# Layer norm of a convolution module: the channel tiles are added on GpSimd and VectorE, and TensorE sums one tile over the partitions instead of eight

## The chip, the core and the metric

The kernel runs on one core of one Trainium2 chip. The metric is device microseconds from the start to the end of one execution, the median of several runs. The profile is one execution of its own, recorded by the hardware profiler; its times are microseconds from the start of the span.

## What is computed

The reference is a decoder trunk of two layers on one sequence of 512 positions and 1024 channels. Layer 0 mixes state-space heads and attention heads; layer 1 is a causal convolution module; each ends in a gated FFN. The change touches the convolution module of layer 1 alone:

```python
def layer_norm(x, g, b):
    mu = jnp.mean(xf, -1, keepdims=True)
    var = jnp.mean(jnp.square(xf - mu), -1, keepdims=True)
    y = (xf - mu) * lax.rsqrt(var + EPS)
    return y * g + b

def conformer_conv(h, w1, b1, w_dw, b_dw, ln_g, ln_b, w2, b2):
    a, gt = jnp.split(h @ w1 + b1, 2, axis=-1)
    u = a * jax.nn.sigmoid(gt)
    u = causal_depthwise_conv(u, w_dw, b_dw)          # 31 taps
    u = jax.nn.silu(layer_norm(u, ln_g, ln_b))
    return u @ w2 + b2
```

The mean and the variance run over the 1024 channels of each position.

## The kernel before, in words

Everything is held transposed: a tile has 128 channels in its partitions and positions along its free dimension, so 1024 channels are eight tiles k = 0 to 7. A sum over channels is a sum over the partitions and over the eight tiles. Positions are handled in two halves of 256, called H0 (positions 0 to 255) and H1 (256 to 511); a name that ends in `_0` or `_256` belongs to one of them.

Products with weights keep float32 accuracy by splitting: `slab` (L181 to L196) loads 1024 x 256 weights as `raw`, ScalarE rounds them to `hi`, and VectorE or GpSimd takes the rest as `lo`; `products` (L198 to L211) issues hi x hi, lo x hi and hi x lo for each tile. `raw`, `hi` and `lo` have two buffers each, so the slab after next waits until TensorE has finished with a slab, and its DMA until the subtraction has read the old `raw`. A plain float32 matmul stands as two passes in the trace; the names `mu`, `var`, `cps` and `lnr_b` below are of this kind.

The module runs like this. For each pair of channel tiles two slabs of the first matrix (`wp`) are multiplied, ScalarE takes the sigmoid, VectorE forms the gated tile `cu`. SP's DMA queue then writes 16 shifted pieces of it (`shifted`, L948 to L951) into a tile `u`; the queue carries the slab loads in between, in the order of the code. `conv` (L953 to L963) is 32 small matmuls per tile into `cps`, and ScalarE moves the result with its bias to `cv`. The conv of tile k - 2 is issued with tile k; the second halves of tiles 4 to 7 follow after the layer norm of H0 in the code. GpSimd builds the filters (`w`, L914) and, for the slabs of H0 of the second matrix, the `lo` part (`wq_l`, L195).

`layer_norm(c)` (L991 to L1015) works on one half. TensorE multiplies each of the eight `cv` tiles by a constant matrix with 1/1024 everywhere (`meanw`) and accumulates, so that `mu` holds the mean in all partitions (L995). VectorE subtracts it from each tile (L999), ScalarE squares (L1003, into `cvq`), and TensorE sums every square tile over its partitions, two blocks of 128 positions each, into a column `var` (L1005). VectorE then computes the reciprocal root with twelve small operations (L221 to L226, L1008) and a diagonal (L271), TensorE spreads it over the partitions (`lnr_b`, L274), VectorE scales (L1012), ScalarE applies SiLU (L1013) and converts to `ch` (L1014), and VectorE forms the rest `cl` (L1015). `pw2` (L1019 to L1025) multiplies by the second matrix in four slabs per half (`wq`, result `pq`), VectorE adds the result to the residual `xT` (L592) and ScalarE and others gather squares for the next norm (`n3`, sums `n_s`, spread `n_b`). The last FFN begins with `first_banks`: gate and up products of its first slabs (`f_a`, `f_b` from `wf`), first for H0, then for H1.

The order in which an engine's instructions stand is not the order of the code alone: the program is recorded and a list scheduler with a model of the time places each engine's instructions. An edit can so move work that it does not name. On the chip each engine works through its list in order.

## Time and profile before

| | |
|---|---|
| median of 3 runs | 1872.89 us (1870.29 to 1874.12) |
| the profiled execution | 1885.09 us |
| its span in the trace | 1882.8 us |
| TensorE busy | 1774.7 us, 94% of the span |
| VectorE busy | 1046.5 us, 56% |
| ScalarE busy | 693.1 us, 37% |
| GpSimd busy | 430.5 us, 23% |
| mean clock granted to TensorE | 0.972 of full speed |

PE is TensorE's matmuls and PEld its weight loads, DVE is VectorE, ACT ScalarE, POOL GpSimd, SP the engine whose queue issues most DMAs. A busy share is an average over the whole kernel; what an edit in the convolution module is worth is read in its own stretch, about 1290 to 1520 us. The clock granted to TensorE is a share of full speed: 1.00 is 2.4 GHz, 0.50 is 1.2 GHz, and a value between is a mean over a stretch that holds both.

### The profile page before, as it was taken

To read this page: it belongs to the slowest core of one execution; us is meant where nothing else is said; L and a number is where in the kernel's file an instruction comes from. 1 tells how busy PE (TensorE), PEld (TensorE's weight loads), DVE (VectorE), ACT (ScalarE), POOL (GpSimd) and SP (SyncE) were. 2 spreads that over 40 slices of the span, in tenths; PEclk is the share of its full clock that TensorE was granted. 3 is DMA by queue.
4 is the path that set the end of the run, shared out by engine and by line. 5 is a ranking of instruction groups with operands and counts; after the bars stand their busy time and mean duration, and the time that the engine had idled before them with its cause. 6 is when DMAs were issued, how large, how long until landed. Compare 5 with 4: busy or idle time off the path is not lost.

```text
span 1882.8 us, 24868 instructions
## 1 busy us (share of the span) xinstructions
PE 1774.7 (94%) x9735; PEld 1450.0 (77%) x9735; DVE 1046.5 (56%) x1978; ACT 693.1 (37%) x1331; POOL 430.5 (23%) x328
## 2 busy tenths in 40 slices
PE   5897978999999999997999999999999999999998
PEld 3676766777778878777888888897567988888888
DVE  7858687755565565558665664373204743333336
ACT  6333333334545454344421221253214632122225
POOL 1437686422443440003000000013020200000001
PEclk8998989999999999997999999999998999999999
DMA  8354454545444443424555553253640523322223
GB/s 301 102 138 140 141 141 134 137 112 152 123 128 149 133 125 122 124 74 141 181 190 190 188 201 114 79 169 80 180 132 1 169 77 102 101 89 93 87 94 130
DMA packets 232066, 247.84 MB, mean 132 GB/s; under 512 B 13946, under 2 KB 198076, under 8 KB 231949
## 3 DMA queue, kind: packets, MB, share of 16 engines
q1 hardware_dynamic: 220813, 204.31, 36.6%
q0 software_dynamic: 11136, 41.95, 6.8%
q8 instruction: 77, 1.26, 0.3%
q14 instruction: 40, 0.33, 0.1%
HBM read 228.73 MB, written 8.64 MB: 126 GB/s over the span
## 4 chain that ended last, share of the span: by engine, by line
PE 73%; DVE 11%; DMA 7%; ACT 3%; issue 2%; POOL 2%; SPq 1%; DVEq 0%; ACTq 0%; POOLq 0%
PE fd L207 4%; PE fd L208 4%; PE fd L210 4%; PE fg L208 4%; PE fg L207 4%; PE fu L207 4%; PE fu L208 4%; PE fu L210 4%; PE fg L210 4%; PE cps L959 2%; PE s L717 2%; DMA ar<-a_dram 2%; PE wa L207 1%; PE wa L208 1%; PE wa L210 1%
## 5 line engine op out<-in xcount | busy, mean ns | idle before, releaser
L249 POOL TENSOR_TENSOR n_acc<-n_acc,n_q 128x256 f32<-128x256 f32 x32 | 29.7, 929 | 561.8 <-ACT n_q L245 561.7
L207 PE MATMUL fd<-uh,wd_h 128*128 128x512 f32 (+1 forms) x448 | 148.6, 347 | 0.9 <-DVE xT L592 0.9
L195 DVE TENSOR_TENSOR wf_l<-wf_w,wf_h 128x1024 fp32r<-128x1024 f32 x88 | 106.1, 1241 | 74.4 <-ACT wf_h L194 74.4
L208 PE MATMUL fd<-uh,wd_l 128*128 128x512 f32 (+1 forms) x448 | 147.0, 344 | 0.0
L194 ACT CAST wf_h<-wf_w 128x1024 fp32r<-128x1024 f32 x88 | 87.7, 1048 | 115.7 <-PE fd L210 71.9
L208 PE MATMUL fg<-n_h,wf_l 128*128 128x512 f32 x320 | 126.1, 394 | 2.0 <-DVE wf_l L195 2.0
L207 PE MATMUL fg<-n_h,wf_h 128*128 128x512 f32 x320 | 126.3, 395 | 0.7 <-ACT wf_h L194 0.5
L208 PE MATMUL fu<-n_h,wf_l 128*128 128x512 f32 x320 | 124.7, 390 | 0.0
L207 PE MATMUL fu<-n_h,wf_h 128*128 128x512 f32 x320 | 124.6, 389 | 0.0
L172 POOL TENSOR_TENSOR adap<-adap 128x128 f32<-128x128 f32 (+2 forms) x96 | 103.5, 1082 | 4.7
L869 DVE TENSOR_TENSOR fs<-fs,fu 128x512 f32<-128x512 f32 x40 | 27.5, 688 | 130.2 <-PE fu L210 130.2
L743 ACT ACTIVATE s<-s,nm 128x128 f32<-128x128 f32 x192 | 79.4, 415 | 50.7 <-DVE nm L739 40.4
L194 ACT CAST wd_h<-wd_w 128x1024 fp32r<-128x1024 f32 (+1 forms) x64 | 57.1, 941 | 101.2 <-PE fd L210 80.6
L592 DVE SCALAR_TENSOR_TENSOR xT<-fd,mod,xT 128x512 f32<-128x512 f32 (+1 forms) x64 | 39.1, 615 | 98.1 <-PE fd L210 97.8
L207 PEld LDWEIGHTS fd<-uh,wd_h 128*128 128x128 f32 x448 | 84.1, 188 | 12.0 <-DVE xT L592 1.3
L208 PEld LDWEIGHTS fd<-uh,wd_l 128*128 128x128 f32 x448 | 84.2, 188 | 10.5
L210 PE MATMUL fd<-ul,wd_h 128*128 128x512 f32 (+1 forms) x448 | 91.9, 343 | 0.0
L170 POOL TENSOR_TENSOR adap<-adap,cs 128x1024 f32<-128x1024 f32 x32 | 67.6, 2112 | 90.3 <-DMA adap<-in_ada_w 90.2
L195 DVE TENSOR_TENSOR wd_l<-wd_w,wd_h 128x1024 fp32r<-128x1024 f32 (+1 forms) x64 | 67.7, 1090 | 34.7 <-ACT wd_h L194 34.4
L162 DVE SCALAR_TENSOR_TENSOR adaa<-adaw,cs,adaa 128x512 f32<-128x512 f32 x112 | 84.8, 758 | 2.6
L210 PEld LDWEIGHTS fd<-ul,wd_h 128*128 128x128 f32 x448 | 72.9, 188 | 10.6
L210 PE MATMUL fg<-n_l,wf_h 128*128 128x512 f32 x320 | 79.1, 389 | 0.0
(400 smaller groups left out, 4584.5 us busy)
## 6 DMA issues: line engine op xcount, KB each, us to landing
adaw<-in_ada_w POOLq DMA_DIRECT2D x24, 1024.0 KB, 5.7
wf_w<-in_ffn_w_gate SPq DMA_DIRECT2D x22, 1024.0 KB, 5.2
wf_w<-in_ffn_w_up SPq DMA_DIRECT2D x22, 1024.0 KB
adap<-in_ada_w POOLq DMA_DIRECT2D x32, 512.0 KB, 5.5
wd_w<-in_ffn_w_down SPq DMA_DIRECT2D x16, 1024.0 KB, 5.1
wd_w<-in_ffn_w_down SPq DMA_DIRECT2D x16, 768.0 KB, 4.6
wa_w<-in_hy_w_out SPq DMA_DIRECT2D x20, 512.0 KB, 4.1
u<-cu SPq DMA_DIRECT2D x128, 67.5 KB, 2.0
```

The source lines that it names most:

```text
L162: V.scalar_tensor_tensor(acc, ws[k // 4][:, k % 4, :], cs[:, k:k + 1], acc, op0=ALU.mult, op1=ALU.add)
L170: G.tensor_tensor(w3, w3, cs.unsqueeze(2).broadcast_to([P, KT, P]), op=ALU.mult)
L172: G.tensor_tensor(w[:, 0:n], w[:, 0:n], w[:, n:2 * n], op=ALU.add)
L194: S.copy(hi[:, s:e], raw[:, s:e])
L195: eng.tensor_tensor(lo[:, s:e], raw[:, s:e], hi[:, s:e].bitcast(F32), op=ALU.subtract)
L207: PE.matmul(ps[:, cols], hi[:, o(k):o(k) + P], xh, start=k == 0, stop=False)
L208: PE.matmul(ps[:, cols], lo[:, o(k):o(k) + P], xh, start=False, stop=False)
L210: PE.matmul(ps[:, cols], hi[:, o(k):o(k) + P], acts[k][1][:, cols], start=False, stop=k == nk - 1)
L592: V.scalar_tensor_tensor(xT[m][:, cols], ps[:, cols], mod[l][:, go + m:go + m + 1], xT[m][:, cols], op0=ALU.mult, op1=ALU.add)
L717: marks[hp, 0] = marks[hp, 1] = PE.matmul(ps[:, o:o + 2 * wd].rearrange("p (e w) -> p e w", e=2), q, k, start=True, stop=True)
L743: S.activation(s[:, o:o + wd], s[:, o:o + wd], AF.Exp, bias=nm, accum_out=l)
L959: PE.matmul(ps[g * 32:(g + 1) * 32, :], w4[k][:, g * 8 + m, :], u4[k][:, g, t:t + w], start=m == 0, stop=m == 7)
```

## The change

For the mean, each `cv` tile of channels is added into a tile `csum` (one for each half) as soon as ScalarE has written it: tiles 0 to 4 on GpSimd, 5 and 6 on VectorE. TensorE multiplies only `csum` and tile 7 by `meanw`. For the variance, the square tiles lie in pairs of 128 x 512 with three buffers of their own; VectorE adds the second and third pair onto the first (`vacc`), and TensorE sums `vacc` and the fourth pair over the partitions.

```diff
--- before.py
+++ after.py
@@ -941,7 +941,7 @@
     with tc.tile_pool(name="conf", bufs=2) as conf:
         h = nxt.finish(const, g_mix1, mod[1][:, 0:8], XG)
         w1 = a["cv_w_pw1"][0]
-        cv, u4 = {}, {}
+        cv, u4, csum = {}, {}, {}
 
         def shifted(k, u):
 
@@ -961,6 +961,11 @@
             for c in cols:
                 o = cv[k, c.start] = conf.tile([P, T // 2], F32, tag=f"cv{k}_{c.start}", name=f"cv{k}_{c.start}", bufs=1)
                 S.activation(o, ps[:, c.start - cols[0].start:c.stop - cols[0].start], AF.Identity, bias=bdw[:, k:k + 1])
+                if k == 1:
+                    csum[c.start] = conf.tile([P, T // 2], F32, tag=f"csum{c.start}", name=f"csum{c.start}", bufs=1)
+                    G.tensor_tensor(csum[c.start], cv[0, c.start], o, op=ALU.add)
+                elif 1 < k < KT - 1:
+                    (G if k < 5 else V).tensor_tensor(csum[c.start], csum[c.start], o, op=ALU.add)
 
         for j in range(4):
             ws = [slab([(w1[:, o + j * 256:o + (j + 1) * 256], KT, 256)], f"wp{o}_{j}") for o in (0, D)]
@@ -991,19 +996,24 @@
             n, w = c.start, c.stop - c.start
             nb = w // P
             mb = bank("A", f"mu{n}", (P, w))
-            for i, k in enumerate(range(KT)):
-                PE.matmul(mb, meanw, cv[k, n], start=i == 0, stop=i == KT - 1)
+            PE.matmul(mb, meanw, csum[n], start=True, stop=False)
+            PE.matmul(mb, meanw, cv[KT - 1, n], start=False, stop=True)
             vp = bank("C", f"var{n}", (P, nb))
-            for i, k in enumerate(range(KT)):
+            vacc = None
+            for k in range(KT):
                 t = cv[k, n]
                 V.tensor_tensor(t, t, mb, op=ALU.subtract)
-                if i % 2 == 0:
-                    two = tmp.tile([P, T], F32, tag="st_sq", name=f"cvq{k}_{n}")
-                sq = two[:, i % 2 * w:(i % 2 + 1) * w]
-                S.activation(sq, t, AF.Square)
-                for b in range(nb):
-                    PE.matmul(vp[:, b:b + 1], sq[:, b * P:(b + 1) * P], ones[:, 0:1], start=i == 0 and b == 0,
-                              stop=i == KT - 1 and b == nb - 1)
+                if k % 2 == 0:
+                    two = conf.tile([P, T], F32, tag="cvq", name=f"cvq{k}_{n}", bufs=3)
+                S.activation(two[:, k % 2 * w:(k % 2 + 1) * w], t, AF.Square)
+                if k == 1:
+                    vacc = two
+                elif k in (3, 5):
+                    V.tensor_tensor(vacc, vacc, two, op=ALU.add)
+            for i, sq in enumerate((vacc, two)):
+                for b in range(2 * nb):
+                    PE.matmul(vp[:, b % nb:b % nb + 1], sq[:, b * P:(b + 1) * P], ones[:, 0:1], start=i == 0 and b == 0,
+                              stop=i == 1 and b == 2 * nb - 1)
             vv = tmp.tile([P, nb], F32, tag="st_v", name=f"lnv{n}")
             V.tensor_scalar(vv, vp, 1.0 / D, EPS, op0=ALU.mult, op1=ALU.add)
             rb = spread(rsqrt(vv, nb, f"ln{n}"), nb, f"lnr{n}")
```

The scheduler places the rest anew. Three places matter below. TensorE, from the first matmul of conv 7 for H0 (`cps7_0`) to the sums of squares of H0; before:

```order
L959 MATMUL cps7_0_11069<-u4_7_10964,w4_7_10782 32x256
L995 MATMUL mu0_11104<-cv0_0_10426,meanw_9893 128x256
L995 MATMUL mu0_11104<-cv1_0_10538,meanw_9893 128x256
L959 MATMUL cps7_0_11069<-u4_7_10964,w4_7_10782 32x256
L995 MATMUL mu0_11104<-cv2_0_10666,meanw_9893 128x256
L995 MATMUL mu0_11104<-cv3_0_10778,meanw_9893 128x256
L995 MATMUL mu0_11104<-cv4_0_10906,meanw_9893 128x256
L995 MATMUL mu0_11104<-cv5_0_11014,meanw_9893 128x256
L959 MATMUL cps7_0_11069<-u4_7_10964,w4_7_10782 32x256
L995 MATMUL mu0_11104<-cv6_0_11067,meanw_9893 128x256
L959 MATMUL cps6_256_11273<-u4_6_10856,w4_6_10670 32x256
L959 MATMUL cps7_0_11069<-u4_7_10964,w4_7_10782 32x256 x29
```

and now, the same stretch:

```order
L959 MATMUL cps7_0_11080<-u4_7_10973,w4_7_10790 32x256
L999 MATMUL mu0_11115<-csum0_10540,meanw_9893 128x256
L959 MATMUL cps6_256_11274<-u4_6_10864,w4_6_10676 32x256
L959 MATMUL cps7_0_11080<-u4_7_10973,w4_7_10790 32x256
L959 MATMUL cps6_256_11274<-u4_6_10864,w4_6_10676 32x256 x6
L959 MATMUL cps7_0_11080<-u4_7_10973,w4_7_10790 32x256
L959 MATMUL cps6_256_11274<-u4_6_10864,w4_6_10676 32x256 x4
L959 MATMUL cps7_0_11080<-u4_7_10973,w4_7_10790 32x256 x29
L959 MATMUL cps6_256_11274<-u4_6_10864,w4_6_10676 32x256 x17
L1000 MATMUL mu0_11115<-cv7_0_11113,meanw_9893 128x256
L959 MATMUL cps5_256_11238<-u4_5_10734,w4_5_10546 32x256 x32
L959 MATMUL cps7_256_11310<-u4_7_10973,w4_7_10790 32x256 x16
```

The seven calls of `mu` between the conv pieces have become one on `csum0`, conv of H1's tile 6 (`cps6_256`) fills the places between, and `mu`'s last call stands behind 17 conv calls instead of 22; the sums of squares come later in the list, behind conv 5 and half of conv 7 of H1.

VectorE, from H0's diagonal `lnr0_d` on; before:

```order
L271 TENSOR_SCALAR lnr0_d_11165<-cst_72,ln0_y_11153 128x128 x2
L1012 TENSOR_TENSOR cv0_0_10426<-cv0_0_10426,lnr0_b_11168 128x256
L1012 TENSOR_TENSOR cv1_0_10538<-cv1_0_10538,lnr0_b_11168 128x256
L1012 TENSOR_TENSOR cv2_0_10666<-cv2_0_10666,lnr0_b_11168 128x256
L1012 TENSOR_TENSOR cv3_0_10778<-cv3_0_10778,lnr0_b_11168 128x256
L1012 TENSOR_TENSOR cv4_0_10906<-cv4_0_10906,lnr0_b_11168 128x256
L1012 TENSOR_TENSOR cv5_0_11014<-cv5_0_11014,lnr0_b_11168 128x256
L1012 TENSOR_TENSOR cv6_0_11067<-cv6_0_11067,lnr0_b_11168 128x256
L1012 TENSOR_TENSOR cv7_0_11102<-cv7_0_11102,lnr0_b_11168 128x256
L999 TENSOR_TENSOR cv0_256_10428<-cv0_256_10428,mu256_11351 128x256
```

and now, the same stretch:

```order
L271 TENSOR_SCALAR lnr0_d_11164<-cst_72,ln0_y_11152 128x128 x2
L1005 TENSOR_TENSOR cv0_256_10428<-cv0_256_10428,mu256_11353 128x256
L1005 TENSOR_TENSOR cv1_256_10542<-cv1_256_10542,mu256_11353 128x256
L1005 TENSOR_TENSOR cv2_256_10673<-cv2_256_10673,mu256_11353 128x256
L1005 TENSOR_TENSOR cv3_256_10787<-cv3_256_10787,mu256_11353 128x256
L1005 TENSOR_TENSOR cv4_256_11235<-cv4_256_11235,mu256_11353 128x256
L1005 TENSOR_TENSOR cv5_256_11271<-cv5_256_11271,mu256_11353 128x256
L1005 TENSOR_TENSOR cv6_256_11307<-cv6_256_11307,mu256_11353 128x256
L1005 TENSOR_TENSOR cv7_256_11343<-cv7_256_11343,mu256_11353 128x256
L1022 TENSOR_TENSOR cv0_0_10426<-cv0_0_10426,lnr0_b_11167 128x256
```

The subtraction of H1's mean (`mu256`, eight tiles) has moved ahead of the scaling of H0 (`lnr0_b`). On ScalarE the same place, from the eviction of H1's last conv tile on, reads now:

```order
L963 ACTIVATE cv7_256_11343<-cps7_256_11310,pb_7015 128x256
L1008 ACTIVATE cvq0_256_11358<-cv0_256_10428 128x256
L1008 ACTIVATE cvq0_256_11358<-cv1_256_10542 128x256
L1008 ACTIVATE cvq2_256_11363<-cv2_256_10673 128x256
L1008 ACTIVATE cvq2_256_11363<-cv3_256_10787 128x256
L1008 ACTIVATE cvq4_256_11369<-cv4_256_11235 128x256
L1008 ACTIVATE cvq4_256_11369<-cv5_256_11271 128x256
L1023 ACT_TABLE_LOAD
L1023 ACTIVATE cv0_0_10426<-cv0_0_10426,pb_7015 128x256
L1023 ACTIVATE cv1_0_10538<-cv1_0_10538,pb_7015 128x256
L1024 CAST ch0_11026<-cv0_0_10426 128x256
```

Six squares of H1 (`cvq..._256`) have moved in between the eviction and the table load for SiLU, which followed the eviction directly before.

The third place is the end of `pw2`'s second half, where the last FFN begins. ScalarE before, from the square of residual tile 5 on (`n3_256_q`; `wf1_1_0_h` is the up slab, `n3_h` the normed input of the FFN):

```order
L245 ACTIVATE n3_256_q5_11904<-xT5_221 128x256
L308 ACTIVATE n3_h0_11990<-n3_g0_0_12032,mod1_7001 128x256
L308 ACTIVATE n3_h1_11991<-n3_g0_1_12037,mod1_7001 128x256
L308 ACTIVATE n3_h2_11992<-n3_g0_2_12042,mod1_7001 128x256
L308 ACTIVATE n3_h3_11993<-n3_g0_3_12047,mod1_7001 128x256
L245 ACTIVATE n3_256_q6_11941<-xT6_222 128x256
L306 ACTIVATE n3_g0_4_12052<-xT4_220,g_ffn1_11974 128x256
L194 CAST wf1_1_0_h_12148<-wf1_1_0_w_12146 128x1024 x2
L306 ACTIVATE n3_g0_5_12057<-xT5_221,g_ffn1_11974 128x256
L306 ACTIVATE n3_g0_6_12062<-xT6_222,g_ffn1_11974 128x256
L306 ACTIVATE n3_g0_7_12067<-xT7_223,g_ffn1_11974 128x256
L245 ACTIVATE n3_256_q7_11970<-xT7_223 128x256
```

and now, the same stretch:

```order
L245 ACTIVATE n3_256_q5_11894<-xT5_221 128x256
L245 ACTIVATE n3_256_q6_11931<-xT6_222 128x256
L194 CAST wf1_1_0_h_12138<-wf1_1_0_w_12136 128x1024 x2
L245 ACTIVATE n3_256_q7_11960<-xT7_223 128x256
L308 ACTIVATE n3_h0_11980<-n3_g0_0_12022,mod1_7001 128x256
L308 ACTIVATE n3_h1_11981<-n3_g0_1_12027,mod1_7001 128x256
L308 ACTIVATE n3_h2_11982<-n3_g0_2_12032,mod1_7001 128x256
L308 ACTIVATE n3_h3_11983<-n3_g0_3_12037,mod1_7001 128x256
```

and TensorE now, from the last matmul of `pq` on:

```order
L210 MATMUL pq256_3_1_0_11934<-cl7_11041,wq256_3_h_11899 128x256
L274 MATMUL n3_0_b_12019<-n3_0_d_12016,ones_74 128x128
L256 MATMUL n3_256_s_12062<-ones_74,n3_256_acc_11043 128x1 x2
L256 MATMUL n3_256_s_12062<-ones_74,n3_256_q7_11960 128x1 x2
L207 MATMUL f1_0_a0_12144<-n3_h0_11980,wf0_1_0_h_12130 128x256
L208 MATMUL f1_0_a0_12144<-n3_h0_11980,wf0_1_0_l_12131 128x256
L207 MATMUL f1_0_b0_12145<-n3_h0_11980,wf1_1_0_h_12138 128x256
L207 MATMUL f1_0_a1_12146<-n3_h0_11980,wf0_1_0_h_12130 128x256
L208 MATMUL f1_0_a1_12146<-n3_h0_11980,wf0_1_0_l_12131 128x256
```

The casts of the up slab now stand ahead of the square of tile 7 and of all `n3_h` tiles of H0, and the sums of H1 (`n3_256_s`) ahead of the first gate matmul; before, the first gate matmul followed the last `pq` matmul directly.

## Rows read from the trace of the kernel before

**Rows 1.** The page's chain that ended last: shares of the span by engine.

```profile
PE 73%; DVE 11%; DMA 7%; ACT 3%; issue 2%; POOL 2%; SPq 1%; DVEq 0%; ACTq 0%; POOLq 0%
```

**Rows 2.** Groups by line, 1286 to 1500: count | busy us, mean ns | idle before, releaser.

```profile
L1005 PE MATMUL var<-ones,cvq 128*128 128x1 f32 x64 | 11.0, 293 | 0.0
...
L249 POOL TENSOR_TENSOR n_acc<-n_acc,n_q 128x256 f32<-128x256 f32 x8 | 8.0, 997 | 19.7 <-ACT n_q L245 19.6
...
L999 DVE TENSOR_TENSOR cv<-cv,mu 128x256 f32<-128x256 f32 x16 | 5.5, 415 | 23.1 <-PE mu L995 23.1
```

**Rows 3.** The chain in order of time, 1402 to 1454: start us, us, what.

```profile
1402.83 2.03 DMA u<-cu
...
1405.58 1.06 PE mu L995 x4
...
1410.30 5.77 PE cps L959 x104
1416.06 0.63 PE mu L995 x2
...
1419.41 1.88 PE var L1005 x16
...
1432.23 0.46 PE lnr_b L274 x4
...
1434.63 1.00 ACT cv L1013 x2
1435.62 0.29 ACT ch L1014
...
1445.75 1.50 PE var L1005 x8
```

**Rows 4.** Timeline, layer norm of H0: start us, us, instruction [idle before <-releaser].

```profile
1381.09 0.47 ACT L963 ACTIVATE cv<-cps,pb 128x256 f32<-128x256 f32 x1 [2.93 <-PE cps L959]
...
1387.86 4.74 POOL L195 TENSOR_TENSOR wq_l<-wq_w,wq_h 128x1024 fp32r<-128x1024 f32 x2 [19.50 <-ACT wq_h L194]
...
1416.73 2.74 DVE L999 TENSOR_TENSOR cv<-cv,mu 128x256 f32<-128x256 f32 x8 [23.09 <-PE mu L995]
...
1426.32 0.16 DVE L1008 TENSOR_SCALAR lnv<-var 128x2 f32<-128x2 f32 x1 [6.85 <-PE var L1005]
...
1428.68 0.48 DVE L271 TENSOR_SCALAR lnr_d<-cst,ln_y 128x128 f32<-128x128 f32 x2
...
1430.43 1.28 ACT L1013 ACT_TABLE_LOAD   x1
1433.24 1.09 ACT L1013 ACTIVATE cv<-cv,pb 128x256 f32<-128x256 f32 x2 [1.52 <-DVE cv L1012]
```

**Rows 5.** Windows: us, busy us (instructions) per engine, granted clock, DMA share, GB/s.

```profile
1434.68:1438.40 3.72, 2.21 (x12) 1.60 (x12) 3.72 (x12) 3.72 (x9) 0.00 (x0) 0.99 0.00 0
1438.40:1453.20 14.80, 14.65 (x68) 14.65 (x69) 5.36 (x23) 4.81 (x15) 0.00 (x0) 0.50 0.00 0
1454.00:1456.00 2.00, 2.00 (x14) 2.00 (x13) 0.03 (x1) 2.00 (x4) 1.37 (x1) 0.65 0.01 4
1453.20:1474.21 21.01, 19.64 (x152) 19.00 (x150) 14.15 (x27) 15.21 (x31) 12.84 (x8) 0.95 0.32 101
1474.21:1498.62 24.41, 24.41 (x204) 24.41 (x205) 18.42 (x38) 12.82 (x22) 4.77 (x4) 1.00 0.56 176
```

**Rows 6.** Timeline of `pw2` and the gate of the last FFN.

```profile
1454.63 4.76 POOL L195 TENSOR_TENSOR wq_l<-wq_w,wq_h 128x1024 fp32r<-128x1024 f32 x2 [56.03 <-ACT wq_h L194]
...
1474.21 0.35 PE L207 MATMUL pq<-ch,wq_h 128*128 128x256 f32 x1 [1.28 <-DVE xT L592]
...
1498.99 1.98 ACT L194 CAST wf_h<-wf_w 128x1024 fp32r<-128x1024 f32 x2
...
1513.12 0.39 PE L207 MATMUL f_a<-n_h,wf_h 128*128 128x256 f32 x1 [0.65 <-ACT n_h L308]
```

**Rows 7.** A window at the gate of the first FFN.

```profile
885.00:888.00 3.00, 3.00 (x18) 3.00 (x17) 3.00 (x2) 0.25 (x1) 3.00 (x2) 0.56 0.00 0
```

## The prediction

> **What bounds the kernel now.** I read the page's chain of waits first. TensorE holds 73% of it, VectorE 11%, DMA 7% [rows 1], so an edit pays only where TensorE waits or does work that others could do. The groups by line, over the convolution module, come second: the 128x1 sums of squares (`var`) are 64 matmuls, two passes for each of 32 calls, and VectorE's first subtraction of the mean was preceded by 23.1 us of idling that ended with `mu` [rows 2]. Third comes the chain in order of time through the first layer norm. It enters from the DMA that delivers the shifted copy of channel tile 7, then lies on TensorE: pieces of conv 7 and 6 with pieces of `mu` between them, until `mu`'s last call ends at 1416.69 [rows 3]. The timeline of VectorE and ScalarE says what follows on them [rows 4]. The windows, last, show what cannot be seen in durations: TensorE's clock is granted in full until 1438.4, stands at half (1.2 instead of 2.4 GHz) until about 1455.4 and is full again afterwards [rows 5]. The 1455.4 is worked out: a mean of 0.65 in the window from 1454 to 1456 leaves 0.6 us of it at full clock. The second matrix (`pq`, from `pw2`) begins in exactly that stretch. I cut the windows where a slab of it ends: 1453.20, 1474.21 (the first half's last) and 1498.62 (the second half's).
>
> All sums are made against the profiled execution (1885.09 us, of which 1882.8 are its span). It is 12.2 us above the median of the runs, 1872.89; I carry the difference over.
>
> **Mean of the first half.** Before, 1405.58 to 1416.69 holds seven calls of `mu`, conv work and the eighth call: 11.11 us. After, one call on the sum, 59 conv calls in 118 passes, one call on tile 7. A lone call takes 0.63, and conv passes run at 5.77/104 = 0.0555 us each [rows 3]: 0.63 + 6.55 + 0.63 = 7.8. So `mu` ends at 1413.4, 3.3 us earlier. This needs the sum to be there at 1405.6. GpSimd's last addition for this half waits for tile 4, which ScalarE writes at 1381.1 to 1381.6; a 128x256 addition on GpSimd takes 1.0, and `wq_l`, next in that queue, starts only at 1387.86 [rows 2, 4], so about 5 us of slack cover it. Behind that `wq_l` stands more than its own engine: its end frees the buffer for a slab whose DMA is ahead of tile 7's shifted copies on SP. VectorE's two additions (0.42 each, like the subtraction) are due after tiles 5 and 6, while it idles [rows 2]. GpSimd's other six additions fall into its idle time; I cost all these at nothing, and if the cover were gone each microsecond of lateness would cost one.
>
> **From the mean to the first SiLU.** Eight subtractions run 1413.4 to 1416.1 (2.74). The new 128x512 additions of squares are not in the rows: at least one 256-wide one (0.42), at most two (0.83); I take 0.8, nearest to twice the width, and they end at 1417.7. Three of the four square tiles go to VectorE and the fourth straight to TensorE, so `var` has 8 calls, 16 passes, instead of 32 passes. In TensorE's queue it stands behind 48 conv calls: 1413.4 + 0.5 + 96 x 0.0555 = 1419.2, so the additions are hidden. Sixteen passes took 1.88 [rows 3]: 1421.1. The reciprocal root, from the first small operation to the diagonal's end, is 1426.32 to 1429.16 = 2.84 [rows 4]: 1424.0. Meanwhile TensorE does the last 16 conv calls (0.5 + 1.8), two calls of `mu` for the second half (1.1) and the spread (0.46 [rows 3]): 1425.0. The scheduler now puts the second half's eight subtractions before the first half's scalings on VectorE, and six squares before the table load on ScalarE. The subtractions start at 1424.5 and delay the first scaling until 1427.2; ScalarE's squares end at 1427.0 and its table load, 1.28, formerly hidden in a wait [rows 4], ends at 1428.3. The first SiLU is then at 1428.3 instead of 1433.24: 4.9 us earlier. I allow 4 to 6.
>
> **First slab of the second matrix.** ScalarE hands over a converted tile every 1.29 us (1.00 and 0.29), the first 1.39 after the first SiLU's start (1434.63 - 1433.24) [rows 3, 4], so TensorE idles from 1425.0 to 1429.7. Before the clock fell in the old kernel TensorE had been busy 2.21 of 3.72 us [rows 5]; a gap of 4.7 us is worse, so I expect half clock in or right after it. The Trainium skill ("TensorE: Matmul & The Clock Gate", Part 1, "What's actually happening") says that the lower clock is the default and that activity releases it. This speaks against taking matmuls away; by that rule the end comes as forecast below, without it about 4.5 us earlier, and the trace agrees with the rule.
>
> At half clock a 128x256 call takes 14.65/68 = 0.215 us, at full clock 24.41/204 = 0.12 [rows 5], and eight passes of `var` 1.5 [rows 3]. Tiles 0 to 2 keep ScalarE's pace until 1433.2; then four calls of `var` (1.5), tile 3 (0.9) and the other four (1.5) give 1437.1. The remaining 32 calls are dense. In the old kernel `var` ends near 1449.8 and the clock rises at 1455.4, 5.6 us of dense work later; the same gives 1442.7. By then 26 calls are done, and six at 0.12 end the slab at 1443.4. Before, it ended at 1453.2: 9.8 us earlier.
>
> **Remaining three slabs, and the second half.** They took 21.01 us before [rows 5], with 2.2 us at half clock and a wait of 1.28 before the second half's first matmul [rows 6]. That wait ends through a slab loaded after `wq_l` and goes, as `wq_l` is earlier too. Full-clock work is 144 x 0.12 = 17.3, the second half's spread (0.46) and a small transpose that now stands in it, as I estimate from that, 0.8. But `wq_h` of slab 3 now stands behind two more casts on ScalarE, and GpSimd's `wq_l` (4.76 a slab, 2.38 a half) follows it [rows 6]: a wait of between nothing and 2.4, I take 1.0. Together 19.1; the second half begins at 1462.5 instead of 1474.21: 11.7 us earlier. Its four slabs take 24.41 as before.
>
> **The gate into the last FFN, which gives back.** In the new order the first gate matmul stands behind the second half's sums of squares, and ScalarE has the last of these squares behind both casts of the up slab (1.98, and they wait for the last `pq` matmul [rows 6]). So TensorE waits 1.98 + 0.4 for the square and 0.5 for the first `n_h`: 2.9 us, then another 0.5 at tile 4, whose scaling stands behind the up slab's VectorE work. With 96 calls (11.5) and the spread (0.4) the second half of the gate starts 15.3 after the last `pq`, against 1513.12 - 1498.62 = 14.5 [rows 5, 6]: 0.8 lost. The wait has a second price. At the gate of the first FFN, from 885 to 888, its clock averaged 0.56 although it was busy throughout [rows 7]: 2.6 us at half, 1.3 lost. I take 1.4.
>
> **Sum:** -11.7 + 0.8 + 1.4 = -9.5 us: 1875.6 for an execution like the profiled one, 1863.4 for the median.
>
> **Rivals.**
> - *The clock holds.* Full clock through the gap: tiles at ScalarE's pace to 1433.6, `var` and tiles by 1436, 32 calls at 0.12, slab done near 1439; 4.5 us more gain, 1859. For it: 1434.68 to 1438.40 was granted 0.99 with TensorE busy 59% [rows 5]. Against: it fell right behind that. 10%.
> - *The clock takes longer.* The clock rises one such dense stretch (5.6 us) later, or the gate's stretch is as long as the 17 us around 1438: each microsecond at half clock costs half a one, so 2.8 to 7 less gain, 1866 to 1870. For it: the long form occurred once [rows 5]; against it: a stretch as short as 2.6 us did too [rows 7]. 17% (9% of it with under 3.7 us left, no change).
> - *Slower.* The half clock that begins in the gap lasts through the whole first half of `pw2`, because the thinned-out matmuls around 1430 to 1437 and the waits for slabs never let it rise. About 19 us of full-clock work after 1443 would take 38: 1863.4 + 19 = 1882. It decides once the half clock lasts some 19 us longer than forecast, 33 in all, against 17 in the longest stretch here. 6%.
> - *The sum is late.* GpSimd's additions hold up `wq_l`, and with it SP's copies of tile 7: it needs over 5 us more than the rows give, and to cancel the gain nearly 15. 2%, counted with no change.
>
> Forecast 65%: 5 to 13 us of gain. **Range** 1857.5 to 1869.5: it holds the forecast, most of the first rival and half of the second. Less than 0.2%, 3.7 us, cannot be told from no change here. Faster 0.83 (forecast 0.65, clock holds 0.10, longer clock 0.08), same 0.11, slower 0.06.
>
> **What would show it.** Right: 24 fewer passes of `mu`, 32 fewer of `var`; first subtraction near 1413.4, first SiLU near 1428, first `pq` near 1430; half clock from within the gap to about 1443; second half of `pw2` near 1462; TensorE idle 2 to 3 us before the first gate matmul. Wrong: `mu` waiting for `csum`, `wq_l` of slab 0 later than 1388, a half-clock stretch past 1450, or a shift between the two traces that is made outside 1404 to 1520.

## The result and the profile after

The changed kernel took 1864.26 us in the median of 6 runs (1860.70 to 1865.82), the kernel before 1873.43 beside it (6 runs): a ratio of 0.995, 95% interval 0.9935 to 0.9966, so half a per cent faster and clear of the noise. The forecast was 1863.4. A second series gave 1864.85 (5 runs) against 1875.0, ratio 0.9943 (0.9922 to 0.9963). The profiled execution took 1865.71 us, its span is 1863.9, the mean granted clock 0.976.

The two spans differ by 18.9 us, twice the difference of the medians, so the first question is where the shift arises. The chain in order of time of the changed kernel, through the same stretch (start us, us, what):

```profile
1395.98 2.03 DMA u<-cu
...
1398.15 0.59 PE cps L959 x2
1398.74 0.63 PE mu L999 x2
1399.37 6.66 PE cps L959 x118
1406.03 0.63 PE mu L1000 x2
...
1411.98 1.88 PE var L1015 x16
...
1420.92 1.09 ACT cv L1023 x2
```

The DMA with which [rows 3] begin starts at 1395.98 instead of 1402.83, so 6.85 us are there before the changed stretch. They need not come from the edit: e2 below, whose instructions up to here are those of the kernel before, came to this point 12 us earlier than it did, and the kernel before had 13.6 us more at half clock ahead of it (last section). Distances are therefore measured from a mark, the first conv piece of channel tile 7 (1404.99 before, 1398.15 after; add 6.84 to compare with the forecast's times). Seen from the mark, `mu` ends at 8.5 instead of 11.7 and the first SiLU starts at 22.8 instead of 28.25 [rows 3, 4].

Groups by line of the same stretch, which answer to [rows 2] (count | busy us, mean ns | idle before, releaser; `csum` is the new sum over the channel tiles):

```profile
L1005 DVE TENSOR_TENSOR cv<-cv,mu 128x256 f32<-128x256 f32 x16 | 5.5, 416 | 13.5 <-PE mu L1000 13.5
L1015 PE MATMUL var<-ones,cvq 128*128 128x1 f32 x32 | 5.3, 293 | 0.0
L968 POOL TENSOR_TENSOR csum<-csum,cv 128x256 f32<-128x256 f32 x6 | 4.3, 734 | 16.7 <-ACT cv L963 16.7
L968 DVE TENSOR_TENSOR csum<-csum,cv 128x256 f32<-128x256 f32 x4 | 3.8, 949 | 4.1 <-ACT cv L963 4.0
```

Half of the `var` passes are gone, VectorE waits 13.5 us for `mu` instead of 23.1, and the additions lie behind waits for ScalarE's tiles. The timeline where the gap forms, and further down in `pw2` and at the gate (for [rows 4, 6]):

```profile
1416.85 0.61 PE L274 MATMUL lnr_b<-lnr_d,ones 128*128 128x128 f32 x4
1417.05 2.74 DVE L1005 TENSOR_TENSOR cv<-cv,mu 128x256 f32<-128x256 f32 x8 [0.31 <-PE mu L1000]
1417.56 2.05 ACT L1008 ACTIVATE cvq<-cv 128x256 f32<-128x256 f32 x6 [1.30 <-DVE cv L1005]
...
1419.70 2.73 DVE L1022 TENSOR_TENSOR cv<-cv,lnr_b 128x256 f32<-128x256 f32 x8
1422.36 0.58 PE L207 MATMUL pq<-ch,wq_h 128*128 128x256 f32 x1 [4.91 <-ACT ch L1024]
...
1445.99 3.29 DVE L1025 TENSOR_TENSOR cl<-cv,ch 128x256 fp32r<-128x256 f32 x3
1446.43 5.10 POOL L195 TENSOR_TENSOR wq_l<-wq_w,wq_h 128x1024 fp32r<-128x1024 f32 x2 [1.75 <-ACT wq_h L194]
1449.20 0.47 DVE L592 SCALAR_TENSOR_TENSOR xT<-pq,mod,xT 128x256 f32<-128x256 f32 x1
1449.60 3.10 DVE L1025 TENSOR_TENSOR cl<-cv,ch 128x256 fp32r<-128x256 f32 x2
1449.73 0.39 PE L207 MATMUL pq<-ch,wq_h 128*128 128x256 f32 x1 [1.18 <-DVE xT L592]
1456.40 0.36 PE L207 MATMUL pq<-ch,wq_h 128*128 128x256 f32 x1 [0.78 <-DVE xT L592]
...
1483.13 0.61 PE L256 MATMUL n_s<-ones,n_q 128*128 128x1 f32 x4 [1.84 <-ACT n_q L245]
1494.20 0.61 PE L274 MATMUL n_b<-n_d,ones 128*128 128x128 f32 x4
```

TensorE idles 4.91 us before the first `pq`: VectorE subtracts the second half's mean and ScalarE squares it before the first half's scaling and SiLU. With the old order, in e3 below, 1.93 us of idling are left. The kernel before idled hardly at all there, with six passes of `mu` behind `lnr_b`:

```profile
1434.68 0.39 PE L207 MATMUL pq<-ch,wq_h 128*128 128x256 f32 x1 [0.71 <-ACT ch L1014]
```

Two waits of 1.18 and 0.78 us stand where the kernel before had one of 1.28. The last row of the timeline, the spread of the second half's norm at the gate, is the end mark: 96.05 us from the first mark, against 106.40 before (1511.39), 10.35 less. The windows, for [rows 5]:

```profile
1420.00:1421.00 1.00, 0.00 (x0) 0.00 (x0) 1.00 (x4) 0.99 (x2) 0.00 (x0) 0.97 0.00 0
1421.00:1422.36 1.36, 0.00 (x1) 0.00 (x1) 1.36 (x6) 1.36 (x4) 0.00 (x0) 0.50 0.00 0
1422.36:1434.00 11.64, 11.51 (x50) 10.92 (x51) 6.76 (x25) 5.65 (x15) 0.00 (x0) 0.50 0.01 2
1434.00:1435.00 1.00, 1.00 (x8) 1.00 (x7) 0.48 (x1) 0.00 (x0) 0.00 (x0) 0.71 0.00 0
1480.00:1500.00 20.00, 18.11 (x151) 17.79 (x150) 15.53 (x48) 13.51 (x31) 0.00 (x0) 1.00 0.31 102
```

The clock falls inside the gap, stays at half for 13.6 us (17.1 before) and is full at the gate.

### The profile page after: what moved, and what is told of

The parts are those of the page before. It is cut to its first block, busy times and chain, and to the rows that moved or that the text cites. A ratio compares the mean times of both kernels' runs of the same rounds, so it can differ in the third digit from the quotient of the medians.

```text
span 1863.9 us, 24762 instructions
## 1 busy us (share of the span) xinstructions
PE 1753.9 (94%) x9679; PEld 1434.4 (77%) x9679; DVE 1051.4 (56%) x1986; ACT 692.9 (37%) x1331; POOL 439.7 (24%) x336
## 4 chain that ended last, share of the span: by engine, by line
PE 71%; DVE 12%; DMA 7%; ACT 4%; issue 3%; POOL 2%; SPq 1%; DVEq 0%; ACTq 0%; POOLq 0%
PE fd L207 4%; PE fd L208 4%; PE fd L210 4%; PE fg L208 4%; PE fu L208 4%; PE fu L207 4%; PE fu L210 4%; PE fg L210 4%; PE fg L207 4%; PE cps L959 2%; PE s L717 2%; DMA ar<-a_dram 2%; PE wa L207 1%; PE wa L210 1%; PE wa L208 1%
## 5 line engine op out<-in xcount | busy, mean ns | idle before, releaser
L208 PE MATMUL fd<-uh,wd_l 128*128 128x512 f32 (+1 forms) x448 | 147.0, 344 | 0.0
L208 PE MATMUL fg<-n_h,wf_l 128*128 128x512 f32 x320 | 125.2, 391 | 2.0 <-DVE wf_l L195 2.0
L208 PE MATMUL fu<-n_h,wf_l 128*128 128x512 f32 x320 | 124.7, 390 | 0.0
L208 PEld LDWEIGHTS fd<-uh,wd_l 128*128 128x128 f32 x448 | 84.2, 188 | 10.5
L210 PE MATMUL fu<-n_l,wf_h 128*128 128x512 f32 x320 | 79.0, 389 | 0.0
```

The source lines that it names most:

```text
L208: PE.matmul(ps[:, cols], lo[:, o(k):o(k) + P], xh, start=False, stop=False)
L210: PE.matmul(ps[:, cols], hi[:, o(k):o(k) + P], acts[k][1][:, cols], start=False, stop=k == nk - 1)
```

## The experiments

All kernels in one table. "SiLU" and "end" are distances in us from the first mark to the first SiLU and to the end mark; "half" is the time at half clock between the marks, added up from windows of 1 us. These three are of one profiled execution of each kernel, and only the changed kernel was profiled twice (e10). The median and the ratio to the kernel before, which ran beside each series, are of the runs.

| kernel | SiLU | half | end | median | ratio (95%) |
|---|---|---|---|---|---|
| before | 28.25 | 17.1 | 106.40 | | |
| changed | 22.8 | 13.6 | 96.05 | 1864.26 | 0.995 (0.9935–0.9966) |
| e1 mean only | 22.7 | 17.1 | 100.22 | 1868.11 | 0.9963 (0.9946–0.998) |
| e2 variance only | 29.2 | 23.9 | 106.62 | 1875.88 | 1.0013 (0.9999–1.0027) |
| e3 first half ahead | 19.8 | 6.8 | 91.76 | 1860.04 | 0.9928 (0.9905–0.995) |
| e4 gap filled | 22.8 | 3.4 | 93.52 | 1864.78 | 0.995 (0.9933–0.9967) |
| e5 variance only, first half ahead | 26.2 | 6.8 | 98.45 | 1867.12 | 0.9966 (0.9948–0.9983) |
| e6 sums on VectorE | 24.4 | 17.1 | 97.88 | 1865.73 | 0.9955 (0.9936–0.9974) |
| e7 = e3 with matmuls added | 19.8 | 3.4 | 90.82 | 1861.66 | 0.9929 (0.9903–0.9954) |
| e8 = e7 with var ahead | 19.8 | 0 | 88.43 | 1853.16 | 0.9893 (0.9867–0.9919) |
| e9 = e8 without them | 19.8 | 6.8 | 89.46 | 1860.30 | 0.9916 (0.9893–0.9939) |
| e10 changed, again | 22.8 | 13.7 | 95.95 | 1864.85 | 0.9943 (0.9922–0.9963) |
| e11 = changed, wq_l on VectorE | 22.8 | 13.7 | 93.64 | 1860.13 | 0.9934 (0.991–0.9958) |
| e12 = e8, wq_l on VectorE | 19.8 | 3.4 | 89.30 | 1856.35 | 0.9917 (0.9885–0.9949) |

**e1, e2: each part alone.** e1 keeps the old loop of `var`, e2 the old loop of `mu`. e1's edit of the kernel before, with the additions into `csum` cut (...):

```diff
...
-            for i, k in enumerate(range(KT)):
-                PE.matmul(mb, meanw, cv[k, n], start=i == 0, stop=i == KT - 1)
+            PE.matmul(mb, meanw, csum[n], start=True, stop=False)
+            PE.matmul(mb, meanw, cv[KT - 1, n], start=False, stop=True)
```

e2 takes the same lines, and the additions, back out of the changed kernel.

> Only the mean is taken from the running sum over the channel tiles; the variance is summed by TensorE over all eight tiles of squares, as in the kernel before. Theory (two separate gains): the mean of the first half ends 3.2 us earlier, the variance's 16 matmuls per half stay, so everything from the first SiLU on comes about 3.2 us earlier and the half-clock stretch stays as long as before (17 us): 3 us under the kernel before, about 1870, ratio 0.998. Rival 1 (the whole gain is the earlier mean, since it moves the start of everything): the full 9 us, ratio 0.995. Rival 2 (the gain is only in the variance and the clock): no difference, 1873.

> Only the variance is taken from running sums of the squares; the mean is summed by TensorE over all eight channel tiles, as in the kernel before. Theory (two separate gains): the first SiLU comes about 1.7 us earlier, the half-clock stretch has 48 fewer 128x1 passes at about 0.21 us to hold PE up and ends 4 to 5 us sooner on top: 5 to 6 us under the kernel before, about 1867.5, ratio 0.997. Rival 1 (the mean's earlier end carries it all): within 1.7 us of the kernel before, ratio 0.999. Rival 2 (the two parts are not additive, the variance alone does it): 9 us, ratio 0.995.

The mean alone gave 6.2 us at the end mark, twice the theory; the variance alone nothing. Neither of the theory's sizes held, nor did rival 1 of e1 (the whole gain); e1's half clock stayed at 17.1 us, as its theory had it. e2's time is the one of its rival 1, but e5 below refutes that rival's reason. The "48 fewer passes" of e2's theory are a slip: 32 of the 64 `var` passes go, 16 of them in the first slab of the second matrix. In e1 the second half's `mu` is short too, and four of its passes stand around the first half's `lnr_b`, where the kernel before had sixteen (ten ahead of it, six behind), so `lnr_b` comes 5.8 us earlier, not 3.2. The timeline of e2 shows where its gain went:

```profile
1417.96 0.61 PE L274 MATMUL lnr_b<-lnr_d,ones 128*128 128x128 f32 x4
1418.16 2.40 DVE L1000 TENSOR_TENSOR cv<-cv,mu 128x256 f32<-128x256 f32 x7 [3.10 <-PE mu L995]
1418.67 2.04 ACT L1003 ACTIVATE cvq<-cv 128x256 f32<-128x256 f32 x6 [3.66 <-DVE cv L1000]
1420.48 2.73 DVE L1017 TENSOR_TENSOR cv<-cv,lnr_b 128x256 f32<-128x256 f32 x8
1422.03 1.09 ACT L1018 ACTIVATE cv<-cv,pb 128x256 f32<-128x256 f32 x2
1423.48 0.58 PE L207 MATMUL pq<-ch,wq_h 128*128 128x256 f32 x1 [4.91 <-ACT ch L1019]
...
1447.39 5.44 DVE L1020 TENSOR_TENSOR cl<-cv,ch 128x256 fp32r<-128x256 f32 x3
1453.29 0.58 PE L207 MATMUL pq<-ch,wq_h 128*128 128x256 f32 x1 [3.76 <-DVE xT L592]
```

`lnr_b` is there 2 us earlier than before (25.1 against 27.1 from the mark), and is followed by seven subtractions and six squares of the second half: the same 4.91 us of idling as in the changed kernel. e1 has the old order and idles 1.78:

```profile
1420.45 0.39 PE L207 MATMUL pq<-ch,wq_h 128*128 128x256 f32 x1 [1.78 <-ACT ch L1019]
```

So the suspect was the order, which comes along with the shorter variance. It isn't all that e2 lost: further down three `cl` subtractions took 5.44 us beside two `wq_l` pieces of GpSimd, `xT` stood behind them on VectorE, and TensorE waited 3.76 us for it. The 10.2 us that e2 has more at half clock than the changed kernel come there and later: 6.8 us that begin inside this wait, and 3.4 us shortly before the end mark.

**e3, e5: the first half ahead.** Both put the second half's subtractions behind the first half's scalings, e3 in the changed kernel, e5 in e2 (`scaled` holds the last scaling of the first half, `issue_after` queues an instruction behind another; lines between are cut):

```diff
-                V.tensor_tensor(t, t, mb, op=ALU.subtract)
+                with tc.issue_after(scaled[-1].ins) if scaled else nullcontext():
+                    V.tensor_tensor(t, t, mb, op=ALU.subtract)
...
-                V.tensor_tensor(t, t, rb, op=ALU.mult)
+                sc = V.tensor_tensor(t, t, rb, op=ALU.mult)
...
+            scaled.append(sc)
```

> The changed kernel, with VectorE's eight subtractions of the second half's mean queued behind the eight scalings of the first half (and so ScalarE's squares of the second half behind the SiLU's table load). Theory: the scalings start 2.65 us earlier, at lnr_b, the table load is no longer behind six squares, and the first SiLU comes about 2 us earlier; PE's idle stretch of 5 us shrinks to 3 us. At least 2 us below the changed kernel, about 1862, ratio 0.994 to the kernel before. If the shorter idle stretch also keeps the clock at full: 3 to 5 us more, 1858 to 1859. Rival: the 16 pieces of the second half (subtractions, squares) now fall between the first half's SiLUs and casts on ScalarE and VectorE and push the last casts back by 8 squares x 0.36 = 2.9 us: no gain, 1864, or 1 us slower than the changed kernel.

> The variance alone from running sums (as the variance-only kernel), with VectorE's subtractions of the second half queued behind the scalings of the first half, which is where the kernel before had them. Distances are from the first conv piece of channel tile 7 to the first SiLU and to the spread of the second half's norm at the gate (before: 28.25 and 106.40 us; variance only: 29.18 and 106.62). Theory (the variance-only kernel lost what it had gained to the order on VectorE and ScalarE): the first SiLU comes 2 us ahead of before, at 26.2, and with 48 fewer passes at half clock the spread comes at 101 to 102; the time is 4 to 5 us under the kernel before, ratio 0.9975. Rival (the 16 matmuls of the second half's mean ahead of the spread of 1/sigma hold the first SiLU, so the order on VectorE does not matter): first SiLU at 28 to 29, the time of the kernel before.

e3 reached the end mark 4.3 us before the changed kernel, more than its theory's 2, since the half clock shrank too (to 6.8 us), though less than the 5 to 7 named for a clock that stays full. Its rival, squares in ScalarE's way and no gain, is refuted. e5 in the same place of the timeline as e2:

```profile
1428.61 0.61 PE L274 MATMUL lnr_b<-lnr_d,ones 128*128 128x128 f32 x4
1429.25 2.74 DVE L1020 TENSOR_TENSOR cv<-cv,lnr_b 128x256 f32<-128x256 f32 x8 [3.54 <-PE lnr_b L274]
1429.71 1.09 ACT L1021 ACTIVATE cv<-cv,pb 128x256 f32<-128x256 f32 x2 [2.75 <-DVE cv L1020]
1431.15 0.39 PE L207 MATMUL pq<-ch,wq_h 128*128 128x256 f32 x1 [1.93 <-ACT ch L1022]
```

Scaling follows `lnr_b` at once, the first SiLU stands at 26.2 as expected, and the end mark comes at 98.45, ahead of the 101 to 102 expected: the variance alone is now worth 7.95 us instead of nothing. Of the 8.2 us between e2 and e5, 3.0 are there at the first SiLU; the rest goes with 17 us less at half clock and with the wait of 3.76, in whose place e5 has 0.42 and 1.89. With that order the parts add up: 6.2 (e1) and 7.95 (e5) make 14.1, e3 has 14.6. The change as made has 10.35: with the order that it brought on VectorE and ScalarE it is 4.3 short.

e1 and e3 also say what the shorter variance does to the clock. Both have the old order and idle 1.78 and 1.93 us before the first `pq`; they differ in the sums of squares, and the half clock lasts 17.1 us in e1 and 6.8 in e3. So in the changed kernel, with 13.6, the shorter variance takes half clock away and the order gives part of it back.

**e4: the gap filled.** `lnr0` is the last matmul of the first half's `lnr_b`.

```diff
+fb = bank("B", "fill", (P, T // 2))
+with tc.issue_after(lnr0.ins):
+    for i in range(11):
+        PE.matmul(fb, meanw, csum[H1.start], start=True, stop=True)
```

> The changed kernel, with 11 additional matmuls (128x256 fp32, some 0.43 us each at full clock, their result is not used) on TensorE between the spread of the first half's 1/sigma and the first product of the second pointwise convolution, where PE is idle for 4.9 us. Theory (the idle stretch lets the clock fall): the granted clock holds at full through the first slab, whose PE work then takes half as long and is bound by ScalarE's casts (last one 5.6 us after the first product) : the first slab ends 4 to 5 us earlier, 1859.5 to 1860.5, ratio 0.993. Rival 1 (the clock falls anyway, since PE waits for a cast of 1.29 us per tile in the first slab): the fall comes later, the same time as the changed kernel within 1 us, 1864. Rival 2 (the additional matmuls stand in the way): 1 to 2 us slower than the changed kernel, 1866.

The added matmuls in the timeline and, below, windows over them and what follows:

```profile
1425.85 4.91 PE L1049 MATMUL fill<-csum,meanw 128*128 128x256 f32 x22
```

```profile
1425.84:1430.90 5.06, 4.92 (x24) 4.00 (x22) 5.06 (x16) 4.75 (x11) 0.00 (x0) 1.00 0.00 0
1430.91:1436.00 5.09, 3.97 (x30) 3.57 (x30) 3.21 (x8) 5.09 (x14) 0.00 (x0) 1.00 0.01 3
1436.00:1440.00 4.00, 4.00 (x23) 4.00 (x23) 3.33 (x18) 0.57 (x2) 0.00 (x0) 0.58 0.00 0
```

With the gap busy the clock is full where the changed kernel had half; it falls only after the sparser stretch that follows (3.97 of 5.09 us busy), for 3.4 us. So the gap brought 10.2 of the changed kernel's 13.6 us at half clock. A gap of that size isn't needed for a fall: the kernel before idled 0.71 us and then worked 2.21 of 3.72 us [rows 5], and its clock fell for 17.1 us. The price is smaller than expected, too: 2.5 us at the end mark, not 4 to 5. The later fall is the one that rival 1 named, though not with its time. In the median nothing shows; 2.5 us would be a ratio of 0.9937, inside the interval.

**e6: who adds.**

```diff
-(G if k < 5 else V).tensor_tensor(csum[c.start], ...)
+V.tensor_tensor(csum[c.start], ...)
```

> The changed kernel, with all additions of the channel sum on VectorE (GpSimd has none of them). Theory (the additions are hidden on either engine): the same distances as in the changed kernel, 22.8 to the first SiLU and 96.05 to the spread, within 0.5; time within 2 us of the changed kernel, 1864. Rival (VectorE is held up in the first matrix of the module, where it splits the weights, or GpSimd's share helped): slab weights late, 1 to 4 us slower than the changed kernel.

1.8 us later at the end mark, but this execution had 3.4 more us at half clock inside the conv stretch, 0.8 us behind the first mark, which costs 1.7 at most; the rest is 0.1, and the median is within 2 us. So no effect of the engine is seen; whether that stretch comes with the edit, one execution can't say.

**e7, e8, e9: clock and root.** e7 is e3 with 4 matmuls in the gap and one behind each of seven SiLUs; e8 lets `cl` matmuls of the first slab follow the second half's `var`; e9 is e8 without added matmuls. e7's matmuls and e8's edit, with lines between cut (`layer_norm.var` is the last matmul of `var`):

```diff
+            for i in range(4):
+                PE.matmul(fb, meanw, csum[H1.start], start=True, stop=True)
+            for k in range(KT - 1):
+                PE.matmul(fb, meanw, cv[k, H0.start], start=True, stop=True)
...
+                with tc.issue_after(behind[0].ins) if behind else nullcontext():
+                    PE.matmul(ps[:, cols], hi[:, o(k):o(k) + P], acts[k][1][:, cols], start=False, stop=k == nk - 1)
...
+                    behind[:] = [layer_norm.var] if c is H0 and j == 0 else []
```

> The kernel with the first half's scalings ahead (first SiLU at 19.8, spread at 91.76 from the first conv piece of tile 7, 6.8 us at half clock), plus 4 additional matmuls (128x256 fp32, result not used) in PE's idle stretch of 1.9 us and one behind each of seven SiLUs. Theory (the half clock is a matter of how little TensorE does in and after the idle stretch, and the dense stretch behind it is bound by TensorE): no half clock before 1440, the first slab bound by ScalarE's casts (last one at about 28 from the start), its end at 32 instead of 34.5, the spread 2 to 3 us earlier, 89 to 90; time 1857.5 to 1858.5. Rival (the additional matmuls cost what they give, some 0.43 us each, 11 of them): spread at 91.5 to 93, time 1860 or more.

> The kernel of the run before this one, with the second half's var matmuls queued ahead of the cl matmuls of the first slab instead of among them. In the run with the first half ahead the reciprocal root of the second half lay beside GpSimd's wq_l pieces, three of its 128x2 operations took 2.39, 2.32 and 0.65 us instead of 0.16, and TensorE idled 1.97 us before the spread lnr_b. Theory (VectorE's small operations are stretched only while GpSimd works): the root ends before wq_l begins, its operations take 0.16 to 0.17 us each, the wait of 1.97 goes, the spread at the gate comes 1.5 to 2 us earlier than in the run without this, 87.5 to 88.5; time 1856. Rival (the wait only moves to the next product's weights, as wq_l is the bound there): the same distance within 0.5 us.

> The last kernel without its 11 additional matmuls: first half's scalings ahead, second half's var matmuls ahead of the cl matmuls. Distances from the first conv piece of tile 7 to the spread at the gate so far: 91.76 with the first half ahead, 90.82 with the additional matmuls too, 88.43 with all three. Theory (the two effects add up): half clock for 6.8 us from about 1.5 us after the first product, as without the additional matmuls; the root of the second half is clear of GpSimd's wq_l and the wait of 1.97 is gone; spread at 89.3 to 89.8, time 1854 to 1857. Rival 1 (the position of var does it all, the clock matters nothing where ScalarE sets the pace): spread at 88.4, as with the additional matmuls. Rival 2 (with the clock at half, the first slab ends later, the root stays ahead but the wait returns at the next slab): 91 to 92.

What e8 is made against stands in e3's timeline:

```profile
1434.23 0.16 DVE L226 SCALAR_TENSOR_TENSOR ln_y<-ln_t,ln_y 128x2 f32<-128x2 f32 x1
1434.40 4.75 POOL L195 TENSOR_TENSOR wq_l<-wq_w,wq_h 128x1024 fp32r<-128x1024 f32 x2 [35.51 <-ACT wq_h L194]
1434.43 2.39 DVE L224 TENSOR_TENSOR ln_t<-ln_y 128x2 f32<-128x2 f32 x1
1436.85 2.32 DVE L225 SCALAR_TENSOR_TENSOR ln_t<-ln_t,lnv 128x2 f32<-128x2 f32 x1
...
1440.91 0.68 PE L274 MATMUL lnr_b<-lnr_d,ones 128*128 128x128 f32 x4 [1.97 <-DVE lnr_d L271]
```

An operation on two elements a row takes 2.39 us because it starts 0.03 us after a GpSimd piece, and ends with it; TensorE then waits 1.97. In e8 the root is done before GpSimd starts (timeline, and windows of the first slab):

```profile
1428.62 0.16 DVE L229 SCALAR_TENSOR_TENSOR ln_y<-ln_t,ln_y 128x2 f32<-128x2 f32 x1
1428.82 2.63 DVE L274 TENSOR_SCALAR lnr_d<-cst,ln_y 128x128 f32<-128x128 f32 x2
1428.90 4.84 POOL L195 TENSOR_TENSOR wq_l<-wq_w,wq_h 128x1024 fp32r<-128x1024 f32 x2 [34.51 <-ACT wq_h L194]
```

```profile
1420.00:1424.00 4.00, 3.55 (x26) 2.94 (x25) 3.35 (x9) 3.37 (x11) 0.00 (x0) 1.00 0.02 4
1424.00:1428.00 4.00, 4.00 (x36) 4.00 (x36) 2.09 (x10) 0.93 (x3) 0.00 (x0) 1.00 0.00 0
```

Only `lnr_d` is still caught (2.63 instead of 0.48), TensorE's wait is gone, and the clock is full between the marks. Placing `var` gave 2.4 (e7 to e8) and 2.3 us (e3 to e9), the added matmuls 0.9 (e3 to e7) and 1.0 (e9 to e8). So between the marks the two effects add up, as e9's theory had it, and e8's distance is the one expected. e7's own theory (2 to 3 us, no half clock) failed: 0.9 us, with 3.4 us at half clock left. The medians don't resolve steps of this size: e3, e7 and e9 lie within 2 us of each other, e9 over the 1854 to 1857 expected for it, and e8 lies 7 us under e9, where the marks have 1.0. e8 is the fastest kernel, 20.7 us under the one before by the medians and 18.0 by the marks, and its interval lies clear of the changed kernel's second series. That the added matmuls keep its clock full every time isn't shown: e7, and e12, which is e8 with one more edit, had 3.4 us at half clock with the same matmuls. e9, without matmuls whose result is not used, is the plainer one at 0.9916.

**e10: the changed kernel again.**

> The changed kernel once more, beside the run before this one on the same chip, for a direct comparison. Theory: 9 us under the kernel before, ratio 0.995, 9 to 11 us above the kernel with the three edits; from the first conv piece of tile 7 to the spread at the gate 96.05, plus 1.7 for each additional 3.4 us at half clock. Rival (the half clock of 13.4 us in the first slab was an accident of that one execution): less than 7 or more than 17 us at half clock there.

95.95 and 13.7 us at half clock: the distance repeats within 0.1 us, and the long half clock came both times, which refutes the rival. By the medians the changed kernel is 11.7 us above e8, by the marks 7.5; the 9 to 11 named lie between.

**e11, e12: without GpSimd's wq_l beside pw2.** e11 edits the changed kernel, e12 e8, in the same way; both move the `lo` part of slabs 2 and 3 of the first half to VectorE.

```diff
-                         G if c is H0 else V)
+                         G if c is H0 and j < 2 else V)
```

> The changed kernel, with wq_l (the low part of the weights) of the first half's slabs 2 and 3 made on VectorE instead of GpSimd. In the changed kernel VectorE's cl subtractions (0.42 us each elsewhere) took 3.29 us for three and 3.10 for two beside GpSimd's wq_l pieces of 2.5, and the two waits of TensorE in the second matrix, 1.18 and 0.78, ended with VectorE's xT behind them. Theory (VectorE is held while GpSimd reads two tiles): without GpSimd's pieces no cl takes longer than 0.5, wq_l takes 2 x 1.45 on VectorE, both waits shrink to under 0.5, the spread at the gate comes 1.5 us earlier than the 96.0 of the changed kernel, 94.5. Rival (VectorE's own 5.8 us more work fill the place of the stretched ones, 6.4 - 2.1 = 4.3): the spread within 0.5 us of 96.0 or later, up to 97.5.

> The kernel with the first half's scalings ahead, the 11 additional matmuls and var ahead of cl (spread at the gate 88.43 from the first conv piece of tile 7, 1853), with wq_l of slabs 2 and 3 on VectorE as well. TensorE has no wait over 0.4 us left between its first product and the gate there. Theory: nothing to gain for TensorE, the spread within 0.5 us of 88.4, time within the spread of the runs of 1853. Rival 1 (VectorE, with 5.8 us more work, delivers cl and xT of the second half later): 1 to 3 us slower. Rival 2 (no stretched operations, so xT comes earlier): 0.5 to 1.5 us faster.

The timeline of VectorE in e11, at the `cl` subtractions that had been stretched:

```profile
1435.35 2.16 DVE L1025 TENSOR_TENSOR cl<-cv,ch 128x256 fp32r<-128x256 f32 x6
...
1438.29 2.90 DVE L195 TENSOR_TENSOR wq_l<-wq_w,wq_h 128x1024 fp32r<-128x1024 f32 x2
```

Six take 2.16 us, where in the changed kernel three took 3.29 and two 3.10; neither of TensorE's two waits is left; the end mark comes 2.4 us earlier, of which the waits are 2.0. The edit takes away two things at once, GpSimd's work beside `cl` and the queue in which `wq_l` stood. Which of them held TensorE is read from the changed kernel's rows: both waits ended with `xT`, and no matmul of `wq_l` (L208) waited. e12 came 0.9 us later than e8, with 3.4 us at half clock that e8 did not have, and 3 us later in the median with overlapping intervals: no gain there, and whether a loss stays open.

## Why the prediction was right

- *Mean of the first half.* 3.3 us earlier forecast, 3.2 measured: `mu` never waited for the sum. VectorE's additions were priced at 0.42 each; one of the four took 2.52 (from 1389.70, while GpSimd worked on `wq_l`), which the slack before 1398.74 covered.
- *To the first SiLU.* 4.9 forecast, 5.5 measured; the spread ended 0.7 earlier than I had it (1424.3 with the 6.84 added, against 1425.0). The order of the second half's subtractions and squares had been read rightly from the order of the instructions, and priced as 2.7 on the first scaling. What the prediction did not see is that this order is what stands between this change and the 14.6 us of e3.
- *First slab.* Half clock from within the gap to 1442.7 forecast; 1427.8 to 1441.4 measured, and the slab ended 10.2 earlier instead of 9.8. That the gap makes the clock fall this early is shown by e4; by how much the shorter variance cuts the stretch is seen between e1 and e3. The clock rose 4.4 us after the last `var` of the slab (1430.2 to 1434.6), where 5.6 had been carried over from the old kernel. The rival in which the clock holds did not come by itself; it was priced at 4.5 more, and e4, which made most of it come, got 2.5.
- *Remaining slabs.* This term was mis-sized: one wait of 1.0, measured 1.18 and 0.78, so the second half of `pw2` started 11.0 earlier instead of 11.7. The forecast put the wait down to `wq_l` being late in GpSimd's queue. The trace shows VectorE's `cl` held beside `wq_l` and `xT` behind them, and in e11 both waits are gone.
- *Gate.* From the last `pq` to the end mark 13.47 us against 12.61: 0.86 given back, 0.8 forecast, and the first gate matmul stands 2.9 behind the last `pq`, as forecast. The second price, 1.4 for a falling clock, did not come: 1.00 from 1480 to 1500, and no half clock there in the second execution either. The step that failed is "The wait has a second price". It rested on a short reading as well: the window of [rows 7] ends at 888, while the trace has half clock from 885.4 to 888.8 and again from 892.2 to 899.0, so the "stretch as short as 2.6 us" lasted 3.4 and was not alone.

At the end mark these make 10.35, where the forecast had 10.9 without the clock's part at the gate and 9.5 with it. The medians' 9.2 and 10.2 can't tell the two apart. That the sum came out so near is in part luck: the price that did not come (1.4) and the waits that were too small (0.7) pull in opposite directions. Of the 18.9 us between the two spans, 6.85 came earlier, 10.35 in the stretch, and 1.7 is a half-clock stretch that only the profiled execution of the kernel before had at 1527.

## What to carry to other kernels

Work taken off the engine that bounds a stage also changes which of two ready pieces the scheduler takes first on the other engines; read that order at the point where the bound engine then waits, since here it cost 4.3 of 14.6 us and, with a collision of VectorE and GpSimd, hid one of the two parts. A gap in TensorE's work can be paid twice, once as idle time and once as half clock behind it (10.2 us of it here, worth 2.5); but a stretch that is only sparse did it as well in the kernel before. Test the parts of a change alone, and where runs differ by several us, compare distances between two marks around the edit rather than whole times.

## What the hardware showed beside this

Some VectorE operations stood still beside GpSimd, others did not. 128x2 operations with two tile inputs took 2.39 and 2.32 us instead of 0.16 (e3), the second ending at 1439.17, where GpSimd's pieces end at 1439.15, and `lnr_d`, with one tile input, 2.63 instead of 0.48 (e8). `xT`, which takes one operand from PSUM, kept its 0.47 at 1449.20 in the changed kernel, beside a `wq_l` that ran to 1451.5. The Trainium skill ("SBUF — State Buffer", "Who interferes with whom") says that a VectorE instruction with two SBUF inputs contends with a GpSimd instruction that reads SBUF, as does one in a two-port mode, and that whoever issues first holds the shared ports for the whole instruction while the other fully blocks. The rows of the 128x2 operations and of `xT` agree; whether `lnr_d` ran in a two-port mode no row here shows.

The first mark itself was reached between 1388.2 and 1406.7 us in fourteen profiled executions, e2 at 1392.9 and the kernel before at 1405.0 with the same instructions ahead of it, while the distance between the marks repeated within 0.1 us in the one kernel that was profiled twice. Part of that spread is half-clock stretches that come in one execution and not in another: ahead of its mark the kernel before spent 81.9 us at half clock and the changed one 68.3. That is not all of it, since e2 also spent 68.3 and was 5.3 us earlier than the changed kernel.
